# State space layer: halves of the states swapped by a product with a permutation, cosine products on VectorE, one split for both directions

## The chip, the cores and the metric

The kernel runs on one core of a Trainium2 chip. A core has TensorE (PE; its weight loads, PEld, overlap the products), VectorE (DVE), ScalarE (ACT), GpSimd (POOL) and SyncE (SP, which issues the transfers). The metric is the device time of one execution in microseconds; lower is better.

## The reference, cut to what matters

Two layers run one after the other. The first one adds a windowed attention branch and a state space branch. The state space branch has 512 channels in 32 groups, 64 complex states for each group, and runs over 2048 positions in both directions (d = 0 forward, d = 1 backward):

```python
for d in range(N_DIRS):
    lam = lax.complex(a_re[d], a_im[d])
    a_bar = jnp.exp(lam * dt)
    bu = lax.complex(einsum('sbgc,gpc->sbgp', ut, real(b_bar)),
                     einsum('sbgc,gpc->sbgp', ut, imag(b_bar)))
    _, xs = lax.associative_scan(_scan_op, (a_el, bu), reverse=(d == 1), axis=0)
    y = y + einsum('sbgp,gcp->sbgc', real(xs), c_re[d]) \
          - einsum('sbgp,gcp->sbgc', imag(xs), c_im[d])
```

The second layer (another attention, a recurrent branch and 32 experts) follows and is not touched by the change.

## The kernel before, in words

The sequence is cut into 128 chunks of 16 positions. Inside a chunk everything is a product with small matrices made ahead; from chunk to chunk a recurrence over 128 steps is left, for each group and direction. A tile `E` of 128 partitions holds the ends of the chunks: real parts of the 64 states in partitions 0 to 63, imaginary parts in 64 to 127, and 2 directions x 2 groups x 128 chunks = 512 columns. A complex recurrence is made real by turning the states: `E` is multiplied with a turning factor (cosine and sine tiles), a real scan with the decay runs over the chunks (`Z`), and the result is turned back (`rt`). Each turn needs x*cos plus or minus (the other half of x)*sin, so the real and imaginary halves have to change places.

`s5_stream` runs over 16 blocks of two groups in a software pipeline: iteration i loads block i (`s5_load`: angles, sine and cosine, chunks of the input turned by TensorE, `uf`, `uh`, `ul`) and makes its chunk ends (`s5_ends`), turns and scans block i-1 (`s5_scan`), turns it back and splits it into a high and a low part for the products (`s5_states`, `xh` and `xl`), and makes the output of block i-2 (`s5_output`, with matrices `T` and `G` that are loaded from memory). Every fourth block a group of channels is complete and four rounds of `s5_turn` and `s5_gelu` follow (`y`, `ys`, `yo`).

Before, `s5_swap` (L1039) multiplied with the sine and swapped the halves in two VectorE instructions on 64 partitions each; the product with the cosine ran on GpSimd, in place; and the split was done once for each direction.

`weave` (L330) writes other work between these steps, since TensorE would wait otherwise: the last tiles of the input projection and the branch product of the attention (`first_branch`, tiles `fm`, `g`, `g0e`). Each step of the stream yields a cost, and `RATIO2` times this cost of other products is written behind it. In this part TensorE and ScalarE run in the order in which the program is written (`manual_schedule`); the order on VectorE, GpSimd and SyncE is set by a scheduler. `branch_operand` (L445) loads four pieces `f` of the attention output (two buffers) and splits each into `h` high and low; there are four such groups of four in `first_branch`.

PSUM has two banks for the use `tr`, which the turned input chunks, the turned outputs and, after the change, the swapped states share.

Of the kernel before, what the change touches and what calls it, by code (L numbers as in the profile page):

```python
# [11 lines left out]
F32 = mybir.dt.float32  # L12
# [4 lines left out]
OP = mybir.AluOpType  # L17
# [3 lines left out]
P = 128  # L21
# [9 lines left out]
def f32(ap):  # L31
    return ap.bitcast(F32)
# [28 lines left out]
class Kernel:  # L61
# [120 lines left out]
    def pool(self, ctx, name, side="left", tags=()):  # L182
        return Pools(self.tc, ctx, name, tags, side=side)
# [16 lines left out]
    def p1(self):  # L200
        tc, nc, a = self.tc, self.nc, self.a
        pool = self.pool
        w_in = a["w_in"][0]
        x = a["x"][0]
        with ExitStack() as ctx:
# [57 lines left out]
            with ExitStack() as c1:  # L263
# [28 lines left out]
                with ExitStack() as c2:  # L292
                    up, mo = pool(c2, "up", "right"), pool(c2, "mo", "right")
                    u = self.u_load(up, wp, w_in)
# [35 lines left out]
            def weave(main, ratio, first=0.0):  # L330

                nonlocal debt
                debt += first
                with tc.manual_schedule(engines={mybir.EngineType.PE, mybir.EngineType.Activation}):
                    for cost in itertools.chain([0.0], main):
                        debt += ratio * cost
                        while debt > 0.0:
                            c = next(fill, None)
                            if c is None:
                                debt = min(debt, 1.0)  # L340
                                break
                            debt -= c
# [13 lines left out]
                weave(self.attn_stream(pool(c1, "ap", "right")), self.RATIO, 15.0)  # L356
            with ExitStack() as c1:

                sp = pool(c1, "sp", "right", "kk xh0 xh1 xl0 xl1 ang cos sin dec E rot_t ub we ug uh ul uf Z rt T G yb y ys yo".split())
                self.s5_setup(sp)  # L360
                weave(self.s5_stream(sp), self.RATIO2, 10.0)
                for _ in fill:
                    pass
# [81 lines left out]
    def branch_operand(self, bp, nm, src, t, bufs, place=None):  # L445

        if place is None:
            hi = bp.tile([P, 4, 512], F32R, name=nm + "h", bufs=bufs)
            lo = bp.tile([P, 4, 512], F32R, name=nm + "l", bufs=bufs)
            place = [(hi[:, k], lo[:, k]) for k in range(4)]  # L450
            copy = self.nc.scalar.copy
        else:
            copy = self.nc.vector.tensor_copy
        for k in range(4):
            f = bp.tile([P, 512], F32, name="f", bufs=2)
            self.nc.sync.dma_start(f, src[k * P:k * P + P, t * 512:t * 512 + 512])
            hi, lo = place[k]
            copy(hi, f)
            (self.nc.gpsimd if copy == self.nc.vector.tensor_copy or k % 2 else self.nc.vector).tensor_tensor(lo, f, f32(hi), OP.subtract)
        return place  # L460

    def branch_tile(self, bp, i, t, j, w, x, bufs, use="mm", tag=""):
# [463 lines left out]
    def s5_setup(self, sp):  # L926
        nc = self.nc
        self.sp5 = sp
        kk = sp.tile([P, P], F32, name="kk")
        nc.gpsimd.iota(kk, pattern=[[1, P]], base=0, channel_multiplier=0, allow_small_or_imprecise_dtypes=True)  # L930
        self.kk = kk
        self.xh = [sp.tile([P, 2, 2, 130], F32R, name=f"xh{i}") for i in range(2)]
        self.xl = [sp.tile([P, 2, 2, 130], F32R, name=f"xl{i}") for i in range(2)]
        for t in self.xh + self.xl:
            nc.vector.memset(f32(t[:, 0, :, 0:1]), 0.0)
            nc.vector.memset(f32(t[:, 1, :, 128:129]), 0.0)
# [98 lines left out]
    @staticmethod  # L1035
    def flat(t):
        return t.rearrange("p d g k -> p (d g k)")

    def s5_swap(self, out, x, sin):  # L1039

        for o, i in ((0, 64), (64, 0)):
            self.nc.vector.tensor_tensor(self.flat(out)[o:o + 64], self.flat(x)[i:i + 64], self.flat(sin)[i:i + 64], OP.mult)

    def s5_scan(self, u):
        nc = self.nc
        flat = self.flat
        E = u["E"]
        Z, rt = u["Z"], u["rt"] = [self.sp5.tile([P, 2, 2, P], F32, name=n, bufs=b) for n, b in (("Z", 1), ("rt", 2))]
        self.s5_swap(rt, E, u["sin"])
        nc.gpsimd.tensor_tensor(E, E, u["cos"], OP.mult)  # L1050
        nc.vector.tensor_tensor(rt, rt, E, OP.add)
        df, Zf, tf = flat(u["dec"]), flat(Z), flat(rt)
        nc.vector.tensor_tensor_scan(Zf[:, :256], df[:, :256], tf[:, :256], 0.0, op0=OP.mult, op1=OP.add)
        nc.vector.tensor_tensor_scan(Zf[:, 256:][:, ::-1], df[:, 256:][:, ::-1], tf[:, 256:][:, ::-1], 0.0, op0=OP.mult, op1=OP.add)

    def s5_states(self, u):
        nc = self.nc
        flat = self.flat
        b, Z, rt = u["b"], u["Z"], u["rt"]
        self.s5_swap(rt, Z, u["sin"])  # L1060
        nc.gpsimd.tensor_tensor(Z, Z, u["cos"], OP.mult)
        nc.vector.tensor_tensor(rt, Z, rt, OP.subtract)
        xh, xl = self.xh[b % 2], self.xl[b % 2]
        for d in range(2):
            o = 1 - d
            self.split(rt[:, d], xh[:, d, :, o:o + P], xl[:, d, :, o:o + P])

    def s5_output(self, sp, u, i):

# [1332 lines left out]
```

## Time and profile before

| | before |
|---|---|
| median of 3 runs | 3245.45 us (3242.33 to 3246.53) |
| the profiled execution | 3240.0 us, span 3238.2 us |
| mean granted clock of TensorE | 0.971 |
| busy share PE / DVE / ACT / POOL | 92% / 67% / 46% / 28% |
| state space stage | 1000 to 1265 us of the span |

The busy shares are means over stages with different limits. The stage that is changed takes 265 of 3238.2 us, and in it VectorE is far busier than on the mean of the kernel.

### The profile page before, as it was taken

The page shows a single profiled execution, that of the slowest core. Times are in us where ns is not written, and L with a number is a line of the kernel's source. Part 1 is how long each engine was busy: PE and PEld are TensorE (multiplying, and loading weights), DVE is VectorE, ACT ScalarE, POOL GpSimd, SP SyncE. Part 2 cuts the span into 40 slices and gives each one's busy share as a digit, 9 for nine tenths or more (in the row PEclk, how much of TensorE's full clock was granted, in tenths as well). Part 3 has the DMA queues.
Part 4 walks back from the last instruction along what each step waited for, and adds up shares of the span by engine and source line. Part 5 has one row for each costly group of instructions (what it writes and reads, how often), then busy time and mean ns, then how long its engine had stood idle before and what let it go on. Part 6 is the DMA issues. An engine that isn't in the chain of part 4 may idle for free. (4 is left out here: it accounts for less than half of the span.)

```text
span 3238.2 us, 43471 instructions
## 1 busy us (share of the span) xinstructions
PE 2990.6 (92%) x14254; PEld 2399.5 (74%) x14254; DVE 2183.7 (67%) x4596; ACT 1500.7 (46%) x2962; POOL 909.7 (28%) x869
## 2 busy tenths in 40 slices
PE   7999999989998788998999789899999997999998
PEld 5778779978886677787888567688778875666665
DVE  4355764448886996637666689988886767674463
ACT  4332332046665544315555677756553424452242
POOL 0003550012223441444443454122210003342232
PEclk9999999999998899999999899999999998999999
DMA  5533557663736878685443531222235328996682
GB/s 170 187 81 136 187 183 235 214 160 110 207 104 186 255 236 259 199 290 161 134 140 119 160 101 47 68 73 85 82 115 198 139 98 305 289 347 197 166 269 48
DMA packets 411126, 545.43 MB, mean 168 GB/s; under 512 B 73953, under 2 KB 263745, under 8 KB 409826
## 3 DMA queue, kind: packets, MB, share of 16 engines
q1 hardware_dynamic: 392850, 508.41, 49.0%
q0 software_dynamic: 18000, 33.60, 4.7%
q8 instruction: 142, 2.33, 0.3%
q14 instruction: 134, 1.10, 0.1%
HBM read 393.00 MB, written 180.84 MB: 177 GB/s over the span
## 5 line engine op out<-in xcount | busy, mean ns | idle before, releaser
L99 PE MATMUL fm<-h,wh 128*128 128x512 f32 x960 | 387.8, 408 | 8.2 <-ACT ev L236 6.2
L100 PE MATMUL fm<-h,wh 128*128 128x512 f32 x960 | 383.8, 400 | 0.0
L101 PE MATMUL fm<-h,wl 128*128 128x512 f32 x960 | 381.5, 398 | 0.6 <-DVE wl L92 0.6
L99 PEld LDWEIGHTS fm<-h,wh 128*128 128x128 f32 x960 | 182.8, 191 | 47.7 <-ACT ev L236 8.2
L101 PEld LDWEIGHTS fm<-h,wl 128*128 128x128 f32 x960 | 182.4, 190 | 41.1 <-DVE wl L92 1.0
L100 PEld LDWEIGHTS fm<-h,wh 128*128 128x128 f32 x960 | 183.0, 191 | 31.9
L99 PE MATMUL mm<-wegh,xh 128*128 128x512 f32 x376 | 169.1, 450 | 17.0 <-PEq L2236 6.9
L2367 PE MATMUL mm<-wd,st 128*128 128x512 f32 x368 | 171.6, 610 | 9.2 <-ACTq L2275 5.3
L2345 ACT ACTIVATE g<-mm 128x256 f32<-128x256 f32 x47 | 18.0, 383 | 297.0 <-PEq L2275 96.4
L2312 DVE TENSOR_TENSOR wegl<-wf,wegh 128x1024 fp32r<-128x1024 f32 x128 | 151.0, 1221 | 3.2
L92 DVE TENSOR_TENSOR tl<-tr,th 128x512 fp32r<-128x512 f32 (+2 forms) x204 | 130.8, 644 | 30.8 <-ACT th L91 29.8
L101 PE MATMUL mm<-wegh,xl 128*128 128x512 f32 x376 | 147.9, 393 | 0.9 <-issue 0.9
L100 PE MATMUL mm<-wegl,xh 128*128 128x512 f32 x376 | 146.9, 391 | 0.0
L863 POOL TENSOR_TENSOR q<-q,q 64x512 fp32r<-64x512 f32 x32 | 43.4, 1355 | 362.5 <-ACT q L862 283.9
L91 ACT CAST th<-tr 128x512 fp32r<-128x512 f32 (+2 forms) x204 | 110.1, 548 | 42.5 <-PE pj L101 18.3
L2367 PEld LDWEIGHTS mm<-wd,st 128*128 128x128 f32 x368 | 68.0, 195 | 82.0 <-issue 66.4
L2311 ACT CAST wegh<-wf 128x1024 fp32r<-128x1024 f32 x128 | 127.6, 1048 | 0.0
L99 PEld LDWEIGHTS mm<-wegh,xh 128*128 128x128 f32 x376 | 70.9, 188 | 53.3 <-issue 33.1
L2346 DVE SCALAR_TENSOR_TENSOR g<-g,mm 128x256 f32<-128x256 f32 x47 | 19.8, 421 | 131.9 <-ACT g L2345 129.2
L99 PE MATMUL mm<-wo,mxh 128*128 128x512 f32 x256 | 105.1, 411 | 2.9 <-ACT mxh L1939 2.9
L100 PE MATMUL mm<-wo,mxh 128*128 128x512 f32 x256 | 103.6, 405 | 0.0
L2369 POOL DMA_INDIRECT out_y<-y,lsidx x32 | 51.6, 1613 | 183.6 <-DVEq L2236 115.7
(700 smaller groups left out, 9071.3 us busy)
## 6 DMA issues: line engine op xcount, KB each, us to landing
wf<-in_w_gate SPq DMA_DIRECT2D x64, 512.0 KB
wf<-in_w_up SPq DMA_DIRECT2D x64, 512.0 KB
wd<-in_w_down SPq DMA_DIRECT2D x62, 512.0 KB
wa<-in_w_ada SPq DMA_DIRECT2D x96, 256.0 KB
w<-in_w_in SPq DMA_DIRECT2D x43, 512.0 KB
g_d<-Gs SPq DMA_DIRECT2D x32, 544.0 KB
G<-g_d SPq DMA_DIRECT2D x32, 544.0 KB
x<-in_x SPq DMA_DIRECT2D x32, 512.0 KB
```

Of the source, the lines that this page charges most:

```text
L91: nc.scalar.copy(hi, src)
L92: nc.vector.tensor_tensor(lo, src, f32(hi), OP.subtract)
L99: mm(ps, lh, rh, start=start, stop=False)
L100: mm(ps, lh, rl, start=False, stop=False)
L101: mm(ps, ll, rh, start=False, stop=stop)
L863: nc.gpsimd.tensor_tensor(q[64:], q2[64:], f32(q[64:]), OP.subtract)
L2311: nc.scalar.copy(hi, f)
L2312: nc.vector.tensor_tensor(lo, f, f32(hi), OP.subtract)
L2345: nc.scalar.activation(g, pm[:, :256], AF.Tanh, scale=0.5)
L2346: nc.vector.scalar_tensor_tensor(g, g, 1.0, pm[:, :256], op0=OP.add, op1=OP.mult)
L2367: nc.tensor.matmul(po, st[:, k * P:k * P + P], wts[1][k][:, hs], start=k == 0, stop=k == 1)
L2369: nc.gpsimd.indirect_dma_start(out=self.out, out_offset=bass.IndirectOffsetOnAxis(ap=sidx, axis=0), in_=y, in_offset=None, compute_op=OP.a ...
```

## The change

The halves are now swapped by one product on TensorE: `swap` is the identity with its halves exchanged, a plain 32-bit matrix of 128x128, and the moving operand is the whole `E` or `Z` of 512 columns. VectorE multiplies the result with the sine out of PSUM (a `tr` bank), multiplies with the cosine itself, and adds or subtracts. The split of the states covers both directions in one instruction on each engine. In `branch_operand` the high part is now always made by ScalarE and the low part by VectorE; before, in `first_branch` VectorE made the high and GpSimd the low part.

```diff
--- before.py
+++ after.py
@@ -356,7 +356,7 @@
                 weave(self.attn_stream(pool(c1, "ap", "right")), self.RATIO, 15.0)
             with ExitStack() as c1:
 
-                sp = pool(c1, "sp", "right", "kk xh0 xh1 xl0 xl1 ang cos sin dec E rot_t ub we ug uh ul uf Z rt T G yb y ys yo".split())
+                sp = pool(c1, "sp", "right", "kk swap xh0 xh1 xl0 xl1 ang cos sin dec E rot_t ub we ug uh ul uf Z rt T G yb y ys yo".split())
                 self.s5_setup(sp)
                 weave(self.s5_stream(sp), self.RATIO2, 10.0)
                 for _ in fill:
@@ -448,15 +448,12 @@
             hi = bp.tile([P, 4, 512], F32R, name=nm + "h", bufs=bufs)
             lo = bp.tile([P, 4, 512], F32R, name=nm + "l", bufs=bufs)
             place = [(hi[:, k], lo[:, k]) for k in range(4)]
-            copy = self.nc.scalar.copy
-        else:
-            copy = self.nc.vector.tensor_copy
         for k in range(4):
             f = bp.tile([P, 512], F32, name="f", bufs=2)
             self.nc.sync.dma_start(f, src[k * P:k * P + P, t * 512:t * 512 + 512])
             hi, lo = place[k]
-            copy(hi, f)
-            (self.nc.gpsimd if copy == self.nc.vector.tensor_copy or k % 2 else self.nc.vector).tensor_tensor(lo, f, f32(hi), OP.subtract)
+            self.nc.scalar.copy(hi, f)
+            self.nc.vector.tensor_tensor(lo, f, f32(hi), OP.subtract)
         return place
 
     def branch_tile(self, bp, i, t, j, w, x, bufs, use="mm", tag=""):
@@ -929,6 +926,9 @@
         kk = sp.tile([P, P], F32, name="kk")
         nc.gpsimd.iota(kk, pattern=[[1, P]], base=0, channel_multiplier=0, allow_small_or_imprecise_dtypes=True)
         self.kk = kk
+        self.swap = sp.tile([P, P], F32, name="swap")
+        for o, i in ((0, 64), (64, 0)):
+            nc.vector.tensor_copy(self.swap[:, o:o + 64], self.ident[:, i:i + 64])
         self.xh = [sp.tile([P, 2, 2, 130], F32R, name=f"xh{i}") for i in range(2)]
         self.xl = [sp.tile([P, 2, 2, 130], F32R, name=f"xl{i}") for i in range(2)]
         for t in self.xh + self.xl:
@@ -1036,34 +1036,37 @@
     def flat(t):
         return t.rearrange("p d g k -> p (d g k)")
 
-    def s5_swap(self, out, x, sin):
-
-        for o, i in ((0, 64), (64, 0)):
-            self.nc.vector.tensor_tensor(self.flat(out)[o:o + 64], self.flat(x)[i:i + 64], self.flat(sin)[i:i + 64], OP.mult)
+    def s5_turned(self, x):
+
+        px = self.bank("tr")
+        self.nc.tensor.matmul(px, self.swap, self.flat(x), start=True, stop=True)
+        return px
 
     def s5_scan(self, u):
-        nc = self.nc
+        V = self.nc.vector
         flat = self.flat
         E = u["E"]
         Z, rt = u["Z"], u["rt"] = [self.sp5.tile([P, 2, 2, P], F32, name=n, bufs=b) for n, b in (("Z", 1), ("rt", 2))]
-        self.s5_swap(rt, E, u["sin"])
-        nc.gpsimd.tensor_tensor(E, E, u["cos"], OP.mult)
-        nc.vector.tensor_tensor(rt, rt, E, OP.add)
+
+        px = self.s5_turned(E)
+        V.tensor_tensor(flat(rt), px, flat(u["sin"]), OP.mult)
+        V.tensor_tensor(E, E, u["cos"], OP.mult)
+        V.tensor_tensor(rt, E, rt, OP.subtract)
         df, Zf, tf = flat(u["dec"]), flat(Z), flat(rt)
-        nc.vector.tensor_tensor_scan(Zf[:, :256], df[:, :256], tf[:, :256], 0.0, op0=OP.mult, op1=OP.add)
-        nc.vector.tensor_tensor_scan(Zf[:, 256:][:, ::-1], df[:, 256:][:, ::-1], tf[:, 256:][:, ::-1], 0.0, op0=OP.mult, op1=OP.add)
+        V.tensor_tensor_scan(Zf[:, :256], df[:, :256], tf[:, :256], 0.0, op0=OP.mult, op1=OP.add)
+        V.tensor_tensor_scan(Zf[:, 256:][:, ::-1], df[:, 256:][:, ::-1], tf[:, 256:][:, ::-1], 0.0, op0=OP.mult, op1=OP.add)
 
     def s5_states(self, u):
-        nc = self.nc
-        flat = self.flat
+        V = self.nc.vector
         b, Z, rt = u["b"], u["Z"], u["rt"]
-        self.s5_swap(rt, Z, u["sin"])
-        nc.gpsimd.tensor_tensor(Z, Z, u["cos"], OP.mult)
-        nc.vector.tensor_tensor(rt, Z, rt, OP.subtract)
-        xh, xl = self.xh[b % 2], self.xl[b % 2]
-        for d in range(2):
-            o = 1 - d
-            self.split(rt[:, d], xh[:, d, :, o:o + P], xl[:, d, :, o:o + P])
+        px = self.s5_turned(Z)
+        V.tensor_tensor(self.flat(rt), px, self.flat(u["sin"]), OP.mult)
+        V.tensor_tensor(Z, Z, u["cos"], OP.mult)
+        V.tensor_tensor(rt, Z, rt, OP.add)
+
+        at = [bass.AP(tensor=x.tensor, offset=x[:, 0, 0, 1:].offset, ap=[list(x.ap[0]), [259, 2], [130, 2], [1, P]])
+              for x in (self.xh[b % 2], self.xl[b % 2])]
+        self.split(rt, *at)
 
     def s5_output(self, sp, u, i):
 
```

The yields of `s5_stream` are the same as before, so the work that is woven in stays where it was. The order of the instructions around the new products follows. The first place is TensorE in an iteration of the second half of the stream: `mm<-uf,we` are the chunk ends, `fm` is the woven branch product, and `tr<-Z,swap` is the new product.

```order
L1032 MATMUL mm<-uf,we 128x128 x4
L99 MATMUL fm<-h_167 128x512
L100 MATMUL fm<-h_167 128x512
L101 MATMUL fm<-h_167 128x512
L1032 MATMUL mm<-uf,we 128x128 x4
L99 MATMUL fm<-h_164,h_161 128x512
L100 MATMUL fm<-h_164,h_161 128x512
L101 MATMUL fm<-h_164,h_161 128x512
L1042 MATMUL tr<-Z,swap 128x512
L99 MATMUL fm<-h_165,h_163 128x512
L100 MATMUL fm<-h_165,h_163 128x512
L101 MATMUL fm<-h_165,h_163 128x512
```

TensorE's queue now holds an instruction that needs the scan of the same iteration; before, its next instruction that needed the states was the product with `xh` one iteration later. The second place is VectorE in such an iteration, before the change (L1042 are the half products with the sine, L1053 and L1054 the scan):

```order
L1062 TENSOR_TENSOR rt<-Z,rt 128x512
L1042 TENSOR_TENSOR rt<-E,sin 64x512 x2
L92 TENSOR_TENSOR xl_9572<-rt,xh_9570 128x2x128 x2
L1051 TENSOR_TENSOR rt<-rt,E 128x512
L470 SCALAR_TENSOR_TENSOR g0e<-g0e,fm 128x512
L1053 SCALAR_TENSOR_TENSOR Z<-dec,rt 128x256
L1054 SCALAR_TENSOR_TENSOR Z<-dec,rt 128x256
L1015 COPY uf<-tr 128x256 x2
L1042 TENSOR_TENSOR rt<-Z,sin 64x512 x2
```

The same place on VectorE after the change:

```order
L1052 TENSOR_TENSOR rt<-tr,sin 128x512
L1053 TENSOR_TENSOR E<-E,cos 128x512
L92 TENSOR_TENSOR ul<-uf,uh 128x256 x2
L565 TENSOR_SCALAR trn_rot<-ang 128x512
L1054 TENSOR_TENSOR rt<-E,rt 128x512
L566 TENSOR_TENSOR ang<-ang,trn_rot 128x512
L1056 SCALAR_TENSOR_TENSOR Z<-dec,rt 128x256
L1057 SCALAR_TENSOR_TENSOR Z<-dec,rt 128x256
L467 SCALAR_TENSOR_TENSOR g0e<-g0e,fm 128x512
L1063 TENSOR_TENSOR rt<-tr,sin 128x512
L1064 TENSOR_TENSOR Z<-Z,cos 128x512
```

Before, the turning back of one block and the turning of the next one were interleaved, with GpSimd between them; after, one block goes through scan and back without another block's turn between. The third place is the first of the four groups of branch operands, on ScalarE (old and new rows side by side; the second `L91` row is the split of the states):

```order
 L251 ACTIVATE ev<-fm,bg 128x512
-L91 CAST xh_9569<-rt 128x2x128 x2
-L1090 COPY yb<-po 128x16x16
-L570 ACT_TABLE_LOAD
-L570 ACTIVATE sin<-ang 128x512
-L571 ACTIVATE ang<-ang 128x512
-L572 ACTIVATE cos<-ang,quarter 128x512
+L455 CAST h_160<-f 128x512
+L455 CAST h_161<-f 128x512
+L455 CAST h_162<-f 128x512
+L455 CAST h_163<-f 128x512
+L91 CAST xh_9575<-rt 128x2x2x128
```

And on VectorE after the change, where that group's low parts stand:

```order
L1064 TENSOR_TENSOR Z<-Z,cos 128x512
L1065 TENSOR_TENSOR rt<-Z,rt 128x512
L1015 COPY uf<-tr 128x256 x2
L456 TENSOR_TENSOR h_160<-f,h_160 128x512
L456 TENSOR_TENSOR h_161<-f,h_161 128x512
L456 TENSOR_TENSOR h_162<-f,h_162 128x512
L456 TENSOR_TENSOR h_163<-f,h_163 128x512
L92 TENSOR_TENSOR xl_9577<-rt,xh_9575 128x2x2x128
```

The four copies now stand in ScalarE's queue ahead of the split of the states, and the four subtractions in VectorE's queue ahead of its low part. With two buffers `f` the third piece can be loaded only when the first subtraction is done. In the other groups the subtractions are spread between other instructions.

## Rows read from the trace of the kernel before

**Rows 1.** The page, part 1: busy us, share of the span, instructions.

```profile
PE 2990.6 (92%) x14254; PEld 2399.5 (74%) x14254; DVE 2183.7 (67%) x4596; ACT 1500.7 (46%) x2962; POOL 909.7 (28%) x869
```

**Rows 2.** Stages: length, busy PE, PEld, DVE, ACT, POOL, clock, DMA share, GB/s.

```profile
1000.00:1265.00 265.00, 213.25 (x1177) 180.68 (x1175) 224.73 (x367) 130.85 (x254) 103.73 (x91) 0.90 0.80 239
1100.00:1240.00 140.00, 118.86 (x677) 101.19 (x676) 134.41 (x211) 68.89 (x143) 61.22 (x51) 0.94 0.79 239
```

**Rows 3.** The same view, cut at TensorE's chunk ends: one, seven times two, last iterations.

```profile
1008.20:1015.70 7.50, 6.89 (x33) 5.84 (x33) 3.78 (x8) 1.25 (x4) 1.55 (x4) 0.77 0.61 222
1015.70:1044.00 28.30, 22.23 (x125) 18.99 (x125) 24.73 (x43) 18.47 (x33) 12.23 (x11) 0.88 0.60 177
1044.00:1073.70 29.70, 25.53 (x143) 21.68 (x144) 28.96 (x51) 16.68 (x31) 11.81 (x10) 0.94 0.78 232
1073.70:1110.10 36.40, 22.49 (x120) 19.24 (x119) 33.29 (x53) 24.00 (x45) 18.00 (x15) 0.77 0.96 275
1110.10:1139.00 28.90, 24.21 (x144) 20.32 (x142) 28.54 (x42) 9.53 (x22) 17.44 (x14) 0.99 0.79 232
1139.00:1174.60 35.60, 29.38 (x165) 24.98 (x166) 34.52 (x55) 20.17 (x40) 16.05 (x14) 0.92 0.65 193
1174.60:1200.90 26.30, 23.96 (x144) 20.73 (x143) 25.82 (x45) 10.99 (x26) 11.55 (x12) 0.98 0.93 287
1200.90:1233.00 32.10, 28.02 (x165) 24.14 (x164) 28.62 (x47) 19.54 (x38) 7.31 (x7) 0.95 0.74 228
1233.00:1265.00 32.00, 26.25 (x128) 21.47 (x127) 15.08 (x25) 5.29 (x14) 6.14 (x5) 0.84 0.91 273
```

**Rows 4.** Groups by line, 1000 to 1265 us: busy us, mean ns, idle before.

```profile
L1042 DVE TENSOR_TENSOR rt<-E,sin 64x512 f32<-64x512 f32 x32 | 25.2, 786 | 4.4 <-ACT E L1033 3.7
L1061 POOL TENSOR_TENSOR Z<-Z,cos 128x512 f32<-128x512 f32 x16 | 23.3, 1458 | 52.9 <-DVE rt L1042 35.6 <-DVE dec L997 17.2
L1050 POOL TENSOR_TENSOR E<-E,cos 128x512 f32<-128x512 f32 x16 | 23.2, 1450 | 44.8 <-DVE rt L1042 37.8 <-ACT sin L570 3.8 <-ACT ys L1108 2.4
L92 DVE TENSOR_TENSOR xl<-rt,xh 128x256 fp32r<-128x256 f32 x32 | 22.6, 729 | 1.2 <-ACT xh L91 0.9
L459 POOL TENSOR_TENSOR h<-f,h 128x512 fp32r<-128x512 f32 x14 | 21.2, 1518 | 30.1 <-DVE h L458 25.4 <-PE po L101 4.7
L1051 DVE TENSOR_TENSOR rt<-rt,E 128x512 f32<-128x512 f32 x16 | 13.0, 813 | 0.9 <-POOL E L1050 0.9
L458 DVE CAST h<-f 128x512 fp32r<-128x512 f32 x14 | 6.6, 484 | 8.0 <-PE fm L101 7.9
```

**Rows 5.** The experts' plain 32-bit products: by tile, and in order of time.

```profile
L2367 PE MATMUL mm<-wd,st x368: 592/592/1222, 2720.8 to 3228.5; 128*128 128x512 f32 x184
2802.81 3.60 PE L2367 MATMUL mm<-wd,st 128*128 128x512 f32 x8
```

**Rows 6.** By tile (rt, g0e): duration ns min/median/max, first and last start.

```profile
L92 DVE TENSOR_TENSOR xl<-rt,xh x32: 398/426/1522, 1028.9 to 1253.0; 128x256 fp32r<-128x256 f32 x32
L1042 DVE TENSOR_TENSOR rt<-E,sin x32: 684/687/1692, 1013.0 to 1237.5; 64x512 f32<-64x512 f32 x32
L1051 DVE TENSOR_TENSOR rt<-rt,E x16: 677/690/1397, 1016.8 to 1243.7; 128x512 f32<-128x512 f32 x16
...
L470 DVE SCALAR_TENSOR_TENSOR g0e<-g0e,fm x24: 655/685/690, 1167.3 to 1312.1; 128x512 f32<-128x512 f32 x24
```

**Rows 7.** In order of time, VectorE and GpSimd: start us, us, instruction.

```profile
1155.56 1.50 DVE L568 TENSOR_SCALAR trn_rot<-ang 128x512 f32<-128x512 f32 x1
...
1155.38 2.83 POOL L459 TENSOR_TENSOR h<-f,h 128x512 fp32r<-128x512 f32 x2 [1.03 <-DVE h L458]
```

**Rows 8.** What TensorE waited for, 1000 to 1265 us: total, times, longest.

```profile
PE tr L1097 <- DVE uf L1015: 11.5, 4, 4.2
PE po L99 <- ACT xh L91: 6.0, 2, 5.1
PE po L101 <- DVE xl L92: 5.7, 7, 1.7
```

## The prediction, written before the change was timed

> **What bounds the kernel now.** I read the page first: TensorE is busy for 92% of the span and VectorE for 67% [rows 1]. Taken alone this says that work should be kept away from TensorE. The change lies in one stage, though, and the view of that stage says something else: from 1000 to 1265 us TensorE is busy for 213.25 of 265 us at a mean granted clock of 0.90, VectorE for 224.73; in the middle, from 1100 to 1240 us, VectorE is busy for 134.41 of 140 us and TensorE for 118.86 [rows 2]. So the engine that the kernel as a whole can spare is full here, and TensorE, which bounds the whole, waits.
>
> Next I cut the stage at the places where TensorE computes the chunk ends, one or two iterations to a stretch [rows 3]. The reader is to compare the length with the two busy times. In the third, fifth, sixth and seventh stretch VectorE is within 1.1 us of the length (28.96 of 29.70, 28.54 of 28.90, 34.52 of 35.60, 25.82 of 26.30) and TensorE has 2 to 6 us to spare. In the eighth the two are level, and in the last only TensorE works. The list of TensorE's waits names VectorE's results: 11.5 us before the turned outputs, 6.0 and 5.7 us for the high and low parts of the states [rows 8]; the high part is ScalarE's, but made from what VectorE delivers. Part of VectorE's time is not its own work. At 1155.56 us an instruction took 1.50 us while a GpSimd subtraction ran [rows 7], and the low part of the states has a median of 426 ns and a mean of 729 [rows 4, 6].
>
> **The change part by part.**
>
> *The products on TensorE.* There are 2 products in each of 16 blocks, 32 in all, with a plain 32-bit matrix of 128x128 and 512 moving columns. The trace has the same form in the experts: 184 products stand there as 368 records, two for each, and eight records in a row take 3.60 us, the last of them 0.592 [rows 5]. That is (3.60 - 0.59) / 7 = 0.43 us from record to record, so 0.86 us for a product (not the 592 ns that the row names), and 32 x 0.86 = 27.5 us for all at full clock. No other work is taken from TensorE.
>
> *VectorE's own work.* Out go 64 half products at 687 ns (44.0 us), 32 low parts at 426 ns (13.6) and 16 copies at 484 ns (7.7) [rows 4, 6]. In come 32 products that read PSUM, at 685 ns like the branch product that also reads PSUM (21.9), 32 products with the cosine at 690 ns (22.1), 16 low parts of twice the size and 16 subtractions, both taken at 690 ns (11.0 each) [rows 6]. That is 65.3 us out and 66.0 us in: even. A half product takes as long as a whole one, so the swap on TensorE pays only for the cosine products that leave GpSimd.
>
> *What VectorE no longer suffers.* GpSimd gives up 23.3 + 23.2 + 21.2 = 67.7 of its 103.73 us [rows 2, 4]. What this is worth to VectorE no row shows directly. In eight groups of VectorE the mean is above the median, from the low part of the states, (729 - 426) x 32 = 9.7 us, and the half product, (786 - 687) x 32 = 3.2 us, to the addition, (813 - 690) x 16 = 2.0 us [rows 4, 6]; together they come to some 37 us. 65% of that, GpSimd's share that goes, would be 24 us; since records of neighbours overlap, less of it is lost time. From below I take 0. I choose 18 us, 8% of VectorE's 224.73 us.
>
> The page "SBUF — State Buffer" of the Trainium skill (section "SBUF: two separate sides") has a rule for this: GpSimd and a VectorE instruction with two SBUF inputs hold one port pair in turn, whole instructions long, and the loser stands still. The trace agrees in part: the branch product, which reads PSUM, never took more than 690 ns, the low part of the states up to 1522 [rows 6]. By the rule taken strictly up to all 67.7 us could come back to VectorE, which would lead to the first rival below; the medians say that most instructions beside GpSimd lose nothing.
>
> *ScalarE.* 16 copies are added and 16 splits saved by joining, on an engine that is busy for 130.85 of 265 us [rows 2]: hidden, except where the four copies stand ahead of the split of the states in its queue and wait for a load. That is so once (third place of the order). Behind them the split, VectorE's low part and the next output wait. I put 2 to 3 us on it, from below 0, and let it stand against the slower clock that TensorE may be spared when it idles less; both stay in the range. The new matrix and its two copies at the start are covered by the attention that still runs there.
>
> *The sum.* For each stretch of rows 3 I add 0.86 us for each new product to TensorE (one in the first stretch, three in the last, four in each other), take 8% from VectorE, take the larger, and keep what the stretch has today above its larger one (first latencies, loads, waits by turns). The results are 8.4, 29.2, 29.7, 33.7, 28.0, 33.9, 27.9, 34.9 and 34.6 us. Against today's lengths that is +0.9, +0.9, 0.0, -2.7, -0.9, -1.7, +1.6, +2.8 and +2.6: **+3.5 us**. VectorE stays ahead in the fourth stretch only; in all others TensorE has become the bound, and what the relief brings in the middle is paid back at the end, where VectorE was no bound. With no relief at all the same table gives +8.8 us.
>
> The profiled execution took 3240.0 us, so the sum gives 3243.5 for it; the median of the runs is 5.45 us above that execution, and I forecast **3249 us** against 3245.45. Changes of under 0.2% (6.5 us) are about what a measurement of this kernel can't tell from none.
>
> **The rivals.**
>
> *The bound moves over without its waits (faster).* When VectorE is no longer late, the waits of rows 8 go, and with them half of what each stretch has above its larger engine, and VectorE is nowhere ahead. Then the lengths are TensorE's busy time with the new products plus half of that remainder: 8.1, 27.5, 29.3, 27.5, 27.8, 33.4, 27.6, 33.2 and 31.7 us, together 246 against 256.8, so 3235 us. For it speaks that the stretch with the largest stall, the fourth, is the one with the most GpSimd work (18.00 us) and a clock of 0.77. Against it: in this stretch four rounds of the gelu hang on two banks and two buffers, which the change leaves as they are. It decides if TensorE's idle time in the stage falls from 52 us (265 - 213.25) to under 18, since 265 - 6.5 - 213.25 - 27.5 is 17.8; my sum leaves it 28.
>
> *TensorE stands at its new products (slower).* The swap of `Z` is in TensorE's queue in the same iteration as that of `E`, and the woven products behind it, the next chunk ends and the outputs all wait if VectorE has not finished the scan. Each of the two products also needs one of two `tr` banks, which VectorE or ScalarE must first empty. Until now TensorE met VectorE's results an iteration later. Today's wait of this sort lasts 5.7 / 7 = 0.8 us [rows 8]; one such wait at the swap of `Z` in each of 16 blocks is 13 us on top of the sum, so 3262 us. For it speak the stretches where both engines end within 2 us of one another in my table. Against it: in a plain iteration TensorE needs 13.7 us after the change (27.4 / 2 in the seventh stretch) and VectorE 11.9, so some 1.8 us are there to take up a late hand-over. It decides if these waits pass 0.2 us on the mean, since 16 x 0.2 + 3.5 is 6.7 us.
>
> *The low clock eats the difference.* If TensorE idles as it does today, but in more places, the new products run at half speed in part of the stage and cost up to 1.72 us each; at the 0.90 granted today 27.5 become 30.6 us. This is a few us and lies inside the range.
>
> **How the numbers follow.** My forecast (the bound moves to TensorE and the gains pay for the products, within 6.5 us) gets 0.38. The slower rival gets 0.35: it needs only short waits, and no relief at all already gives +8.8. The faster one gets 0.27. These are the chances of same, slower and faster. The forecast's own range is 3239 to 3252. For 8 in 10 the range reaches below the faster rival by 4 us and above the slower one by 5: 3231 to 3267. All 27.5 us uncovered would be 3273, outside.
>
> **What would show it.** In the profile after: 64 records of the swap product at some 0.43 us from start to start; VectorE's busy time in the stage down by some 18 us with as many us of instructions; the low part of the states at about 690 ns on the mean, near its median; GpSimd down by about 68 us; plain iterations of 13.7 us, bound by TensorE; a shorter stretch around the first and second gelu; the last two stretches longer by 2 to 3 us each. The sum would be wrong if TensorE's list of waits showed the swap products with more than 10 us together, or if VectorE stayed within 1 us of the length in the plain iterations, or if something moved behind 1265 us, where only the order of a few instructions changes.

## The result and the profile after

| | before | after |
|---|---|---|
| median of 5 runs each | 3245.45 us (3241.43 to 3247.16) | 3262.35 us (3259.88 to 3277.41) |
| ratio, 95% interval | | 1.0072 [1.0053, 1.0091]: slower |
| the profiled execution | 3240.0 us, span 3238.2 | 3271.19 us, span 3269.0 |

The profiled execution of after lies 9 us above the median of its runs, so its trace shows more loss than the median does. In what follows the traces say where the time goes, and the ratios say how much it is (0.1% is 3.2 us).

The page's part 1 after, with the columns of [rows 1]:

```profile
PE 3009.0 (92%) x14318; PEld 2400.7 (73%) x14318; DVE 2129.3 (65%) x4582; ACT 1507.2 (46%) x2962; POOL 834.0 (26%) x821
```

VectorE is busy for 54.4 us less than in [rows 1], though its own work was counted as even, and GpSimd for 75.7 us less. The stage after, with the columns of [rows 2]:

```profile
1000.00:1265.00 265.00, 214.58 (x1160) 171.77 (x1158) 171.63 (x337) 131.70 (x243) 31.02 (x45) 0.91 0.72 218
1100.00:1240.00 140.00, 122.57 (x685) 98.65 (x686) 100.94 (x195) 74.09 (x144) 17.20 (x25) 0.95 0.68 208
```

From 1100 to 1240 us VectorE's busy time falls from 134.41 to 100.94 us. It is no bound any more. TensorE's rises only from 118.86 to 122.57 us in the same time, though it has more to do. The stretches from chunk end to chunk end, cut as in [rows 3], without the last one:

```profile
1008.26:1017.07 8.81, 8.42 (x34) 6.99 (x35) 2.29 (x6) 3.75 (x8) 1.78 (x3) 0.73 0.54 194
1017.07:1045.38 28.31, 25.47 (x133) 20.40 (x132) 22.16 (x47) 17.09 (x28) 4.62 (x6) 0.94 0.66 198
1045.38:1077.32 31.94, 28.29 (x151) 22.47 (x150) 22.80 (x46) 16.73 (x28) 4.75 (x6) 0.95 0.61 187
1077.32:1123.08 45.76, 21.26 (x129) 16.64 (x128) 22.83 (x45) 24.24 (x42) 4.18 (x6) 0.78 0.80 238
1123.08:1152.04 28.96, 27.01 (x151) 21.41 (x150) 23.28 (x46) 12.52 (x29) 4.04 (x7) 1.00 0.76 225
1152.04:1181.88 29.84, 29.54 (x173) 24.45 (x172) 23.92 (x47) 18.59 (x35) 3.12 (x6) 1.00 0.53 158
1181.88:1218.79 36.91, 29.31 (x151) 23.66 (x150) 23.83 (x46) 12.76 (x29) 4.45 (x7) 0.86 0.80 254
1218.79:1254.58 35.79, 31.59 (x174) 25.10 (x173) 24.70 (x48) 19.32 (x36) 2.28 (x3) 0.95 0.69 212
```

Together the eight stretches last 246.3 us, against 224.8 before and 225.7 in the forecast. They are 20.6 us longer than forecast, and the fourth (45.76 for 33.7) and the seventh (36.91 for 27.9) account for that: they are 21.1 us too long together. The others are right to within 4.1 us, and their errors cancel. In both bad stretches neither TensorE's nor VectorE's busy time is near the length. The list of TensorE's waits, 1000 to 1289 us, names who was late (total us, times, longest), to be held against [rows 8]:

```profile
PE tr L1100 <- ACT yb L1093: 19.3, 1, 19.3
PE tr L1042 <- DVE uf L1015: 9.7, 8, 3.8
PE tr L1042 <- ACT E L1033: 7.5, 1, 7.5
...
PE tr L1042 <- ACT ev L251: 2.7, 1, 2.7
...
PE tr L1042 <- ACT y L1103: 1.9, 1, 1.9
PE tr L1042 <- DVE Z L1057: 1.5, 3, 0.6
```

The waits for the parts of the states, `xh` and `xl`, have gone from the list. VectorE's copy `uf` is still there with 9.7 us, now ahead of the swap product, and ScalarE's 19.3 us stand at the top. L1042 is the swap product; its five rows come to 23.3 us. The view in order of time shows the 19.3 us, in the fourth stretch (start us, length, instruction, idle before it):

```profile
1082.78 1.06 SPq L453 DMA_DIRECT2D f<-attT  x2
1083.93 1.61 SPq L1082 DMA_DIRECT2D T<-k_d  x2
...
1087.64 6.81 SPq L462 DMA_DIRECT2D g<-tgT  x3
1088.46 0.62 ACT L455 CAST h<-f 128x512 fp32r<-128x512 f32 x1 [6.08 <-DMA f<-attT]
1089.11 0.69 DVE L456 TENSOR_TENSOR h<-f,h 128x512 fp32r<-128x512 f32 x1 [5.57 <-ACT h L455]
...
1094.55 0.85 SPq L453 DMA_DIRECT2D f<-attT  x2
...
1099.89 1.29 ACT L455 CAST h<-f 128x512 fp32r<-128x512 f32 x2 [9.67 <-DMA f<-attT]
1100.54 1.36 DVE L456 TENSOR_TENSOR h<-f,h 128x512 fp32r<-128x512 f32 x2 [9.59 <-ACT h L455]
1101.08 0.61 ACT L91 CAST xh<-rt 128x512 fp32r<-128x512 f32 x1
1101.60 0.37 ACT L1093 COPY yb<-po 128x256 f32<-128x256 f32 x1
...
1102.02 1.12 PE L1100 MATMUL tr<-ident,yb 128*128 128x128 f32 x4 [19.33 <-ACT yb L1093]
```

ScalarE's first copy waits for its load, issued at 1082.78. Two buffers `f` serve four pieces, so the other two loads go out only when VectorE has finished with the first ones, and SP then has three loads `g` ahead of them, whose issue stretches over 6.81 us. The loads leave at 1094.55 and the copies run at 1099.89. Behind them in ScalarE's order stand the high part of the states and the copy `yb` of the output, both of whose inputs had been ready since 1083 us; TensorE stands for 19.3 us. In the trace of before the loads of this group take as long:

```profile
1079.13 0.92 SPq L456 DMA_DIRECT2D f<-attT  x2
...
1085.65 0.42 DVE L458 CAST h<-f 128x512 fp32r<-128x512 f32 x1
1086.15 1.65 POOL L459 TENSOR_TENSOR h<-f,h 128x512 fp32r<-128x512 f32 x1 [0.70 <-DVE h L458]
```

The copy of the third piece ran at 1100.21 us there, as late as the 1099.89 us after. But VectorE shows no idle time before these copies: it had other work, in the order that the scheduler had set. The move put the copies on an engine whose order is that of the program. The Trainium skill ("Perfetto Trace Analysis", section "Tensor Engine Instruction (MATMUL, LD_WEIGHTS)") calls ScalarE, VectorE and GpSimd strict FIFO; the 19.3 us agree for ScalarE.

In the seventh stretch, at the third group of operands, it happens again, with the chunk ends `E` behind the copies (ScalarE, then TensorE):

```profile
1194.91 0.62 ACT L455 CAST h<-f 128x512 fp32r<-128x512 f32 x1 [11.34 <-DMA f<-attT]
1197.06 0.62 ACT L455 CAST h<-f 128x512 fp32r<-128x512 f32 x1 [1.53 <-DMA f<-attT]
1197.59 0.64 ACT L1033 COPY E<-mm 128x256 f32<-128x256 f32 x2
...
1198.28 2.07 PE L1042 MATMUL tr<-E,swap 128*128 128x512 f32 x2 [7.53 <-ACT E L1033]
```

### The profile page after: what moved, and what is told of

It is laid out like the page before. It is cut to its first block, busy times and chain, and to the rows that moved or that the text cites. A ratio compares the mean times of both kernels' runs of the same rounds, so it can differ in the third digit from the quotient of the medians.

```text
span 3269.0 us, 43500 instructions
## 1 busy us (share of the span) xinstructions
PE 3009.0 (92%) x14318; PEld 2400.7 (73%) x14318; DVE 2129.3 (65%) x4582; ACT 1507.2 (46%) x2962; POOL 834.0 (26%) x821
## 5 line engine op out<-in xcount | busy, mean ns | idle before, releaser
L91 ACT CAST th<-tr 128x512 fp32r<-128x512 f32 (+2 forms) x204 | 110.2, 549 | 40.4 <-PE tr L901 17.1
L99 PE MATMUL mm<-woh,mh 128*128 128x512 f32 x240 | 99.4, 415 | 3.5 <-DVE x L1201 3.5
```

The lines of the kernel that those rows point to most:

```text
L91: nc.scalar.copy(hi, src)
L99: mm(ps, lh, rh, start=start, stop=False)
```

## The experiments

Ratios are to before, timed beside each kernel, with 95% intervals, from 5 to 12 executions of each. Gains and losses go by the ratios, since the median of before itself lay between 3240.99 and 3245.45 us when the kernels were timed. "Old operands" are VectorE's copy and GpSimd's subtraction. Lines left out of an edit are marked "...".

### The halves of the change apart

**The change with the old operands** (`operands_back`).

```diff
-            self.nc.scalar.copy(hi, f)
-            self.nc.vector.tensor_tensor(lo, f, f32(hi), OP.subtract)
+            copy(hi, f)
+            (self.nc.gpsimd if copy == self.nc.vector.tensor_copy or k % 2 else self.nc.vector).tensor_tensor(lo, f, f32(hi), OP.subtract)
```

> The changed kernel with the branch operands made as before the change (high part on VectorE, low part on GpSimd); the swap product, the cosine on VectorE and the joint split stay. Theory (the loss is the stall of ScalarE's four copies, which stand in its queue for pieces that are loaded late: 19.3 us idle of TensorE in one place and parts of 7.5 and 3.8 us later): the time falls to 3235 to 3250 us, and the idle stretch of 19.3 us is gone. Rival (the loss is the price of 27.5 us of the swap products and TensorE's waits at them): it stays at 3255 to 3266 us.

Measured: 3253.95 us, 1.0034 [1.0021, 1.0046], between the two ranges. The stall is gone, and about half of the loss. The other half, 0.34% or 11 us, belongs to the swap, the cosine and the split.

**Before with the new operands alone** (`only_operands`): the same lines, the other way round.

> The kernel before with this one part of the change alone: high parts of the branch operands on ScalarE, low parts on VectorE. Theory (stall of ScalarE's queue): 3258 to 3272 us, with an idle stretch of over 10 us on TensorE at the first group of operands. Rival (swap products): 3241 to 3250 us.

Measured: 3252.72 us, 1.0027 [1.0016, 1.0039], again between the two ranges. The move of the operands alone costs 9 us, and the stall is there without any swap product: TensorE stands for 21.4 us before `tr`, behind this copy:

```profile
1102.16 0.62 ACT L455 CAST h<-f 128x512 fp32r<-128x512 f32 x1 [10.27 <-DMA f<-attT]
```

**Before with the joint split alone** (`split_only`).

```diff
...
-        for d in range(2):
-            o = 1 - d
-            self.split(rt[:, d], xh[:, d, :, o:o + P], xl[:, d, :, o:o + P])
...
+        self.split(rt, *at)
```

> The kernel before with this one part of the change alone: one split for both directions. 32 instructions fewer on ScalarE and VectorE, 2 to 3 us less on VectorE, which bounds four stretches: 3238 to 3246 us.

Measured: 3238.47 us, 0.9991 [0.9982, 1.0000]. Of the parts that were run alone it is the only one that doesn't lose, and its ratio is the lowest here; the gain is at the edge of what can be told.

### The operands

**Each group in steps** (`spread`): one load, copy and subtraction at a time, written between the steps of the branch product.

```diff
-        nxt = operand(0)
-        yield self.LAG
...
+        for n, _ in enumerate(operand(0, nxt)):
+            yield self.LAG / 2 if n == 0 else self.LAG / 4
```

> The changed kernel, with each group of four branch operands written out in five steps: the first two loads, then one copy on ScalarE and one subtraction on VectorE at a time, with steps of the stream in between. The engines of the copies and subtractions are those of the change. Theory (the operands' part of the loss is the wait for late loads in a row of four in a fixed order, not the engines): it comes down to the 3254 us of the kernel with the old operands or below, 3246 to 3256 us, and no idle stretch of TensorE over 6 us before a turned output. Rival (ScalarE or VectorE lack the time for the pieces): it stays at 3258 to 3266 us.

Measured: 3258.58 us, 1.0048 [1.0034, 1.0062]. The fourth stretch is back at 33.4 us and the waits of ScalarE for `f` fall from 35.2 to 6.3 us. Yet the time is the rival's: only a part of it comes back, and the interval overlaps with that of the change. The trace is that of the shortest of the six executions (3249.81 us, which lies in the theory's range), so it does not show where the median loses. The engines are those of the change here, so what comes back speaks for the order; no run moved all of the copies, or the subtractions, by themselves.

**The last two pieces of a group copied by VectorE** (`last_two_vector`).

```diff
-            self.nc.scalar.copy(hi, f)
+            (self.nc.scalar.copy if k < 2 else self.nc.vector.tensor_copy)(hi, f)
```

> The changed kernel, but of each group of four branch operands only the first two, which are loaded ahead, are copied by ScalarE; the last two, whose buffer must first come free, are copied by VectorE, whose order the scheduler sets. Theory (it is the wait for the late load in ScalarE's fixed order): 3238 to 3252 us, the idle stretch of 19.3 us down to under 6. Rival (ScalarE's copies as such, or the subtractions on VectorE): 3255 to 3266 us.

Measured: 3261.53 us, 1.0057 [1.0044, 1.0070]: no help that can be told, and a time as the rival had it. TensorE's wait for `yb` did fall from 19.3 to 8.5 us, so an idle stretch that goes from the trace does not come back in the time one for one. VectorE now waits for the late load itself, with its subtractions tied to ScalarE's copies:

```profile
DVE h L455 <- DMA f<-attT: 12.5, 4, 5.7
...
ACT h L455 <- DMA f<-attT: 6.7, 2, 6.1
```

**The first group, or the last, with the old operands** (`first_back`, `last_back`): `old = t == 0`, or `t == 3`.

```diff
-            self.nc.scalar.copy(hi, f)
-            self.nc.vector.tensor_tensor(lo, f, f32(hi), OP.subtract)
...
+            (self.nc.vector.tensor_copy if old else self.nc.scalar.copy)(hi, f)
+            (self.nc.gpsimd if old else self.nc.vector).tensor_tensor(lo, f, f32(hi), OP.subtract)
```

> The change, but the first of the four groups of branch operands (four loads, copies and subtractions, at 1083 us of the stage) is back on VectorE and GpSimd. Theory 1 (the 19.3 us in which all engines stood there are the larger part of what the move of the operands costs): the chunk ends and the outputs no longer stand behind ScalarE's copies at this place, no idle stretch of TensorE over 10 us is left before 1110 us, and the time falls by 5 to 9 us against the change, to 3253 to 3257. Theory 2 (the loads come late whatever waits for them, and the later groups stall in the same way): TensorE's idle time moves to the second and third group, and the time stays at 3259 to 3263.

> The change, but the last of the four groups of branch operands (behind the last block, where the last rounds of the gelu run) is back on VectorE and GpSimd. Theory 1 (ScalarE's four copies stand in its order among the copies of the last outputs, and the stretch from the last load of T to the last yT, 40.2 us against 28.8 before, is longer by that): this stretch falls to 31 to 34 us, and the time by 2 to 6 us against the change, to 3256 to 3260. Theory 2 (the stretch is only longer because the new order of the blocks before it leaves more work there): it stays at 38 to 41 us, and the time at 3261 to 3263.

Measured: 3256.22 us, 1.0046 [1.0033, 1.0059] for the first group; 3263.92 us, 1.0074 [1.0060, 1.0088] for the last. With the first group the time is that of theory 1: with the stall of 19.3 us go 0.26%, some 8 us. The runs (3254.96 to 3257.56) lie below all of `last_back` (3260.61 to 3268.49), which was timed beside it. But the third group's stall stays, as theory 2 had it:

```profile
1183.45 0.62 ACT L457 CAST h<-f 128x512 fp32r<-128x512 f32 x1 [10.39 <-DMA f<-attT]
...
1186.21 0.64 ACT L1035 COPY E<-mm 128x256 f32<-128x256 f32 x2
```

The last group costs no time that can be told. The end of the stage did become shorter, as theory 1 had it (from the last load of `T` to the last store `yT`: 28.8 us before, 40.2 after, 32.6 here), but the time is that of theory 2. Both ends, from the view by tile (the number before the semicolon is the last start), first of before, then of after, then of `last_back`:

```profile
L1079 SPq DMA_DIRECT2D T<-k_d x15: 572/589/599, 1199.6 to 1253.5; - x15
L1115 SPq DMA_DIRECT2D yT<-yo x8: 319/587/1047, 1232.2 to 1282.3; - x8
```

```profile
L1082 SPq DMA_DIRECT2D T<-k_d x20: 579/594/602, 1202.9 to 1277.4; - x20
L1118 SPq DMA_DIRECT2D yT<-yo x8: 320/458/940, 1252.2 to 1317.6; - x8
```

```profile
L1084 SPq DMA_DIRECT2D T<-k_d x19: 579/591/620, 1200.0 to 1273.4; - x19
L1120 SPq DMA_DIRECT2D yT<-yo x8: 319/549/912, 1247.7 to 1306.0; - x8
```

### The swap

**The swapped states in a bank of the use `mm`**: with the old operands (`swap_mm`), in the change (`after_mm`), and in the change with the first group on the old operands (`first_back_mm`).

```diff
-        px = self.bank("tr")
+        px = self.bank("mm")
```

> The changed kernel with the old operands, and the swapped states in a bank of the use mm (which only the chunk ends share) in place of tr. Theory (of the swap's own 11 us a good part is the turn by turn of two tr banks: 12.2 us of TensorE's waits at the swap are for VectorE's copy that empties a tr bank): 3242 to 3250 us, these waits under 4 us. Rival (the 27.5 us of products on TensorE alone): 3251 to 3257 us as without the edit.

> The change, with the swapped states in a bank of the use mm instead of tr. Theory 1 (the turn by turn of the two tr banks and the stall at the operands are two losses that add): 6 us less than the change, as between the two kernels with the old operands (3253.95 and 3247.72), so 3255 to 3258. Theory 2 (the waits for tr banks are taken up by the time that ScalarE's copies lose anyway): within 2 us of the change, 3260 to 3264.

> The change, with the first group of branch operands on the old engines and the swapped states in a bank of the use mm. Theory 1 (the bank was worth nothing in the change because TensorE stood 19 us at the operands anyway; with that stall gone the turn by turn of the tr banks counts again): 4 to 7 us less than with the first group alone (ratio 1.0046), so a ratio of 1.0024 to 1.0034. Theory 2 (it is ScalarE's order, not TensorE's banks, that sets the pace as long as any group of operands is on ScalarE; TensorE then waits for the chunk ends E that ScalarE copies): within 2 us of the first group alone, a ratio of 1.0040 to 1.0052, and TensorE's waits for the tr banks return as waits for E.

Measured: 3247.72 us, 1.0018 [1.0007, 1.0029] with the old operands; 3263.5 us, 1.0068 [1.0053, 1.0082] in the change; 3259.6 us, 1.0061 [1.0045, 1.0077] with the first group back. With the old operands the bank is worth about 5 us (1.0034 without it), at the edge of what can be told, since the two intervals overlap. What goes is this wait for VectorE to empty a `tr` bank of the turned input (`operands_back`):

```profile
PE tr L1045 <- DVE uf L1018: 12.2, 8, 3.4
```

In the change it is worth nothing that can be told (1.0068 against 1.0072). Those waits go there too, but others come (`first_back_mm`):

```profile
PE mm L1044 <- ACT E L1035: 16.2, 4, 9.3
```

The ratio of `first_back_mm` is above what either theory gave, but the waits are those of theory 2: in these traces TensorE waits for ScalarE's `E` in place of the bank as long as ScalarE's order holds copies that wait for loads. No sum of the two losses shows in the times, but the intervals are too wide to rule it out.

**Every swap product twice** (`swap_twice`, old operands): a second one into the same bank.

```diff
+        self.nc.tensor.matmul(px, self.swap, self.flat(x), start=True, stop=True)
```

> The changed kernel with the branch operands as before the change, and every swap product computed twice into the same bank: 32 more products on TensorE and nothing else. If TensorE bounds the iterations after the change, the time is 20 to 28 us above that of the kernel without the doubling; if VectorE still bounds them, less than 10 us above.

Measured: 3270.98 us, 1.0082 [1.0069, 1.0095]: 0.48%, or 16 us, above `operands_back`, for 27.5 us of products, between the two cases. About six tenths of a further product show in the time.

**The products beside the old way** (`products_beside`): the joint split alone, with the 32 products computed and not used, so that VectorE and GpSimd do what they did before.

```diff
...
+        self.nc.tensor.matmul(self.bank("mm"), self.swap, self.flat(x), start=True, stop=True)
         for o, i in ((0, 64), (64, 0)):
```

> The joint split alone (ratio 0.9991), with the 32 swap products computed beside it into mm banks, and not used: VectorE still multiplies the halves, GpSimd the cosine. It has TensorE's price of the change without VectorE's relief. Theory 1 (the products cost TensorE about six tenths of their 27.5 us here, as the second set of them did: 15 to 17 us; and VectorE's relief pays back about half of that, since the kernel with the swap in an mm bank is at 1.0018): 1.0035 to 1.0045. Theory 2 (TensorE idles so much beside the full VectorE that the products hide, and the relief pays nothing): 0.9990 to 1.0020, at or below the swap in an mm bank.

Measured: 3267.48 us, 1.0074 [1.0062, 1.0087]. Both theories fall. Against the joint split alone (0.9991) this is 0.83%, or 27 us: as much as all 27.5 us of the products, beside a TensorE that idles. There is one more wait in this kernel: GpSimd multiplies in place, so it must now wait until the product has read the tile:

```profile
POOL Z L1065 <- PE mm L1044: 28.3, 4, 12.0
```

Little of it reaches VectorE, which waits for these two products of GpSimd for 3.8 and 3.1 us here and for 1.2 and 5.0 us in `split_only`.

### The cosine

**The products with the cosine back on GpSimd**, with the swap in `tr` (`cos_pool`) and in `mm` (`swap_mm_pool`), both with the old operands.

```diff
-        V.tensor_tensor(E, E, u["cos"], OP.mult)
+        self.nc.gpsimd.tensor_tensor(E, E, u["cos"], OP.mult)
...
-        V.tensor_tensor(Z, Z, u["cos"], OP.mult)
+        self.nc.gpsimd.tensor_tensor(Z, Z, u["cos"], OP.mult)
```

> The changed kernel with the old operands, and the cosine products back on GpSimd; the swap stays on TensorE. If VectorE's relief from GpSimd is what the change gains, it loses that: 3256 to 3266 us. If VectorE is no longer the bound, its 22 us of cosine products leave without effect and the time stays at 3250 to 3257 us.

> The old operands, the joint split, the swap as a product in a bank of the use mm, and the products with the cosine on GpSimd as before. Theory 1 (the parts add: the bank is worth 6 us, the cosine on GpSimd 3 us, and the products on TensorE still cost what VectorE's shorter work does not give back): 3244 to 3247, above the joint split alone (3238.5). Theory 2 (once the banks are out of the way VectorE's shorter work pays for the 32 products): 3236 to 3240, as fast as the joint split alone or faster.

Measured: 3250.76 us, 1.0026 [1.0015, 1.0037], and 3250.26 us, 1.0024 [1.0013, 1.0035]. Each interval overlaps widely with that of its partner (1.0034 and 1.0018), so the cosine's engine makes no difference that can be told. `cos_pool` lies at the lower end of the case in which VectorE is no longer the bound; the second kernel is slower than either theory gave. The page's part 1 of `operands_back`, then of `cos_pool`:

```profile
PE 3009.0 (92%) x14318; PEld 2404.4 (74%) x14318; DVE 2142.7 (66%) x4582; ACT 1497.4 (46%) x2946; POOL 857.4 (26%) x837
```

```profile
PE 3012.5 (93%) x14318; PEld 2404.3 (74%) x14318; DVE 2138.9 (66%) x4550; ACT 1498.9 (46%) x2946; POOL 904.9 (28%) x869
```

32 products of 0.69 us left VectorE (22 us), and its busy time fell by only 3.8. So beside 47.5 us more of GpSimd VectorE's other work took 18 us longer. The pair with the bank `mm` shows the same: beside 42.9 us more of GpSimd (857.8 to 900.7) VectorE's busy time fell by 5.5 us (2140.9 to 2135.4), so 17 us were lost. This slowing costs no time that can be told. `swap_mm_pool` differs from `products_beside` in that VectorE multiplies once out of PSUM in place of two halves: 0.50%, or 16 us, less, for 22 us of VectorE's work.

## Why the prediction was wrong

The forecast was no change within 6.5 us. The kernel is slower by 0.72%, outside the forecast's own range (3239 to 3252 us) and inside the wide one (3231 to 3267). Two steps failed: the price of ScalarE's copies, and the cover of the products by TensorE's gaps. The move of the operands alone (0.27%) and the rest of the change (0.34%) add up to 0.61%, inside the interval of the whole.

**ScalarE's copies: the first step that failed.** "I put 2 to 3 us on it", at one place in the order, set against the clock. In the time it is 0.27% (9 us) when it is the only edit, and undoing it takes the change from 1.0072 to 1.0034. In the trace it is 19.3 us at the first group, and 7.5 us at the third, where the prediction saw no such place. The prediction named the right place and the right queue behind it, but priced the copies as if the load were nearly there. That the third load must wait for one of two buffers stands in the section on the change, but the price does not hold it. Two things it missed that the trace of before could show: the first copy runs 6.5 us after its load is issued (1079.13 to 1085.65 us), and the load of the third piece leaves only at 1090.75 us, behind others in SP's queue, for a copy at 1100.21.

**The slower rival was half right.** It gave 3262 us by waits of TensorE at its swap products, and the list shows 23.3 us of these, beyond the 10 us set as the limit; but 7.5 of them are ScalarE's copies again, and the 19.3 us stand elsewhere, so it is luck that its time came out. With the old operands the two `tr` banks that it named cost about 5 us, at the edge of what can be told. Its other wait, for the scan of the same block, is 1.5 us in three times: the early meeting of the two engines did little. In the change as it stands the banks cost nothing that can be told.

**The sum for the stretches comes out without these two, but by luck.** With the old operands and the other bank the ratio is 1.0018, 2 to 9 us, where the sum had +3.5. Two errors cancel in it: the products, with no relief, were to cost 8.8 us and cost 24 (`products_beside`, 1.0074, against before), and the relief was to give back 5 of these and gave back 18 (1.0074 to 1.0018). Plain iterations were forecast at 13.7 us, bound by TensorE; this one is:

```profile
1205.44:1218.79 13.35, 13.29 (x76) 10.79 (x75) 8.71 (x19) 5.12 (x11) 1.79 (x3) 1.00 0.67 213
```

**The products on TensorE: the second step that failed.** They are 64 records, as forecast, and two of them take 1.02 to 1.10 us at the full clock, so the 27.5 us were sized rightly. That the gaps of TensorE would cover most of them without any relief (+8.8 us in the same table) is not borne out: `products_beside` loses 27 us by them. The table let each product fill the time in which TensorE waited. In the traces, over the same 13 iterations (1003.77 to 1212.02 us in `split_only`, 1011.75 to 1235.92 us with the products), TensorE's busy time grows by 22.0 us and its idle time falls only from 41.8 to 35.7 us. Why the gaps do not take up more no run here shows; VectorE's waits for GpSimd explain little of it.

**What VectorE no longer suffers** was put at 18 us, from 0 to 24. The two pairs with the cosine measure it directly: 18 us for 47.5 us of GpSimd and 17 for 42.9, about 0.39 us for each us. For the 67.7 us that leave GpSimd that is an estimate of 26 us, a little above the range. The 54.4 us of busy time are not all of this kind: the joint split alone takes 12.7 us off VectorE (2183.7 to 2171.0) where it was counted as 2.6, with GpSimd's busy time within 3 us of before. The rule of "SBUF — State Buffer" in the Trainium skill (section "SBUF: two separate sides"), that GpSimd and a VectorE instruction with two SBUF inputs hold one port pair in turn, led to at most 67.7 us; taken as a full us for each us it is more than twice what these pairs show. The low part of the states has a mean of 703 ns and a median of 693, where [rows 4, 6] have 729 and 426 for half the size:

```profile
L92 DVE TENSOR_TENSOR xl<-rt,xh 128x512 fp32r<-128x512 f32 x16 | 11.2, 703 | 5.9 <-ACT xh L91 5.9
```

But the faster rival built on it fails: TensorE's idle time in the stage is still 50.4 us (265 - 214.58), not under 18. The prediction said that the swap "pays only for the cosine products that leave GpSimd", which as VectorE's account is right, 22 us saved and 22 spent. In time the two differ: VectorE's two halves made one are worth 16 us, and where the cosine runs makes no difference that can be told.

**Behind 1265 us** the end of the stage is 11 us longer than before. Undoing the last group shortens it in the trace and does not change the median, and why stays open. Open too is why the 19.3 us that go with the first group in the trace are only some 8 us by the ratio. The profiled execution of after was a long one, and so was that of `only_operands` (3259.39 us, where its eleven run from 3244.08 to 3259.57): the stall may differ from one execution to the next, but each kernel has one trace.

## What to carry to other kernels

Before an instruction that waits for a load is moved to an engine that runs in the order of the program, read from the trace of before when its load lands and what stands behind it: the price can be up to that gap, for each pair of buffers, and not the instruction's length. Idle time of an engine is not room that new work fills by itself: a run with the new work alone and none of its gains, as `products_beside` is, measures the price. Relief of an engine need not come back as time, as the cosine shows. Two waits can hide one another, so each has to be undone alone and together with the other to be seen. In an edit of several parts time each part alone: here only the joint split did not lose.

## What was not expected of the hardware

While the engines stood (VectorE and ScalarE were busy for 1.4 of 16 us, the others not at all), the transfers moved 316 GB/s, where the stage has 218 on the mean, and TensorE's granted clock fell to 0.52, close to the lower of its two levels (1.2 of 2.4 GHz):

```profile
1084.00:1100.00 16.00, 0.00 (x0) 0.00 (x0) 1.39 (x2) 1.35 (x3) 0.00 (x0) 0.52 1.06 316
```

After the idle 7.53 us at 1190.74 us the two records of a swap product took 2.07 us in place of 1.02 to 1.10, at a granted clock of 0.50 from 1198.2 to 1200.4 us. Such a stall is paid a second time by the products behind it. The "low clock" of the rivals is there in the bad stretches as a consequence of ScalarE's wait; over the whole stage the granted clock is 0.91, where it was 0.90 before.
